# Two-layer decoder trunk on one core: another order inside the three turns between row-wise sums and the next products

## The chip, the core and the metric

The kernel runs on one core of one Trainium2 chip. The metric is the device time of one execution in microseconds (us). The core has five engines that run on their own and meet at semaphores: PE (TensorE: matrix products and transposes), DVE (VectorE: elementwise work and sums), ACT (ScalarE: activations, copies, square sums), POOL (unused here but for constants) and SP (it issues the DMAs). The "granted clock" in the profile is the share of full speed that PE is given.

## The reference

Two layers, 256 tokens, 2048 columns. Cut to what matters here:

```python
for l in range(DEPTH):
    mod = c_act @ w_ada[l] + b_ada[l]
    shift_a, scale_a, gate_a, shift_m, scale_m, gate_m = split(mod, 6)
    h = rms_norm(x, g_pre_mix[l]) * (1 + scale_a) + shift_a
    y = token_mixer(h, ...)                   # one projection h @ W_in, mLSTM and attention, @ W_out
    x = x + gate_a * rms_norm(y, g_post_mix[l])
    h = rms_norm(x, g_pre_mlp[l]) * (1 + scale_m) + shift_m
    y = square(relu(h @ w_up[l])) @ w_down[l]
    x = x + gate_m * rms_norm(y, g_post_mlp[l])
return x
```

## The kernel before

**Products.** Every weight tile is loaded as float32 (`raw`, by SP's queue, six buffers) and split into a high part (`whi`, an ACT copy to the product format) and a low part (`wlo`, DVE: raw minus high). Activations are kept as high and low parts too (`ht...`). A product is a sum of three: high by high, high by low, low by high. A `Unit` is 512 output columns, accumulated in two PSUM banks; a slab is two 128-row weight tiles of it. `split_hi` and `split_lo` issue the two halves of a split (and first the DMA of a later tile), `take` hands the oldest split slab on.

**Turns.** A turn stands wherever a row-wise norm must be finished before the next product can start: after the output projection (to the up products `up`) in both layers, and after layer 0's down products (to layer 1's `vm` and `kva`). There are three in the run. The 256 tokens are two halves of 128 (`tok` 0 and 1), and PE works on the last columns of half 1 while DVE and ACT finish half 0. For each half the order is:

1. `evac`: the last 512 columns leave PSUM: ACT takes their square sum (`jko`, or `jkd` in the second turn), DVE multiplies by the gate (`yg`; in the second turn it first adds into `ys` and the product goes back into the PSUM bank `dn`). `branch` then makes two more sums over these columns: DVE the product sum of branch and residual, whose elementwise output is thrown away into a spare place (`waste`), ACT the square sum of the branch (`jkb...`).
2. `gain`: the reciprocal root of the branch's mean square: DVE reduces four sums (`sst...`), ACT takes the root (`rp..._y`), DVE makes the reciprocal and one step of Newton's method.
3. `root_after`: from the branch's sums (`sum3...`) the mean square of the new residual, and its reciprocal root (`rn..._y`).
4. `step(c, tok)`: x += branch * root, for 512 columns `c`. `scale`: `xn` = x * root. `group(g, tok)`: four PE transposes of `xn` into a PSUM bank (`pst...`), four ACT shifts and scales (`hf...`), an ACT copy to the high part, a DVE subtraction for the low part.

`group_fast`, used once in each turn, for group 0 of half 1, has two PSUM banks; ACT writes the high part straight from PSUM, DVE makes the shifted value again and subtracts.

While half 1 goes through 1 to 4, PE has the first two slabs of the next unit for half 0, and then products whose result nobody reads (`idle`, here called fillers). In a turn (`strict["on"]`) each engine runs in exactly the order in which the code is written; elsewhere a scheduler, which goes by its own cost estimates, sets the order of each engine.

In the rows `up0_0_1` is layer 0, unit 0, half 1; `pstm0_0_1` the transposes of group 0, half 1; `hi0_3h` and `hi0_3l` (and so `hi_5l` in the profile, where digits are cut) are high and low parts of weight slabs that lie in other pools. Pinned instructions carry the line of the wrapper, L63, so names tell them apart.

Of the kernel before, what the change touches and what calls it, by code (L numbers as in the profile page):

```python
# [39 lines left out]
def hymba_kernel(ctx: ExitStack, tc: tile.TileContext, x_d, c_d, cols_d, cons_d, wada_d,  # L40
# [95 lines left out]
        hold["ada"] = last.ins  # L136
        return y

    def rsqrt_one(ssq, n_over, name):

        h, y, t = [smp.tile([P, 1], F32, tag=f"rs_{a}", name=f"{name}_{a}") for a in "vyt"]
        A.activation(y, ssq, AF.Sqrt, bias=eps, scale=1.0 / n_over)
        V.tensor_scalar(h, ssq, -0.5 / n_over, -0.5 * EPS, ALU.mult, ALU.add)
        V.reciprocal(y, y)
        V.tensor_scalar(t, y, y, h, ALU.mult, ALU.mult)
        V.scalar_tensor_tensor(y, t, 1.5, y, ALU.add, ALU.mult)
        return y
# [195 lines left out]
    class Unit:  # L343
# [23 lines left out]
        def slabs_by_token(self):  # L367
# [3 lines left out]
            for tok in range(2):  # L371
                for s in four:
                    if tok == 0:
                        side()
                    self.mm(s, toks=(tok,))

        def run(self, deep=0):

            self.slabs(self.nk // 2 - deep)
            for _ in range(deep):  # L380
                st["ahead"] += 1
                self.slabs(1)
            st["ahead"] = LA + 1
            return self.ps
# [63 lines left out]
    class PreNorm:  # L448
# [3 lines left out]
            self.tag, self.l, self.vsc, self.vsh, self.yg, self.ssy = tag, l, vsc, vsh, yg, ssy  # L452
            self.xn, self.groups, self.r, self.sums = {}, {}, {}, {}

        def gain(self, tok):

            tot = smp.tile([P, 1], F32, tag="ssq1", name=f"sst{self.tag}_{tok}")
            V.tensor_reduce(tot, self.ssy[:, tok, :], AX.X, ALU.add)
            return rsqrt_one(tot, D, f"rp{self.tag}_{tok}")

        def sums_of(self, tok):
            if tok not in self.sums:
# [73 lines left out]
        def group_fast(self, g, tok, between):

            hh, hl, mods, hf = self.begin(g, tok)
            ps = [xalloc(f"pst{self.tag}_{g}_{tok}_{i}") for i in range(2)]
            pk = [ps[k // 2][:, (k % 2) * P:(k % 2 + 1) * P] for k in range(4)]  # L540
            for k in range(4):
                T.transpose(pk[k], self.xn[g, tok][:, k * P:(k + 1) * P], ident)
            for k, (gc, sc) in enumerate(mods):
                A.activation(hh[:, k, :], pk[k], AF.Identity, bias=sc, scale=gc)
            between()
            for i in range(2):
                kk = slice(2 * i, 2 * i + 2)
                for k in range(2 * i, 2 * i + 2):
                    V.tensor_scalar(hf[:, k, :], pk[k], mods[k][0], mods[k][1], ALU.mult, ALU.add)
                V.tensor_tensor(hl[:, kk, :], hf[:, kk, :], hh[:, kk, :].bitcast(F32), ALU.subtract)  # L550
            xdone(2)

        def begin(self, g, tok):
            tag, l = self.tag, self.l
            ada_until(l, self.vsc, self.vsh, n=4 * g + 4)
# [68 lines left out]
            T.matmul(ps, w[:, 0, 0:P], w[:, 1, :], start=True, stop=True)  # L624
        xdone()

    def turn(units, evac, early, nrm, make, staged=None):

        s0 = st["mm"]
        units[0].slabs(1)
        split_to(s0 + 7)
        rest = []
        for i, u in enumerate(units[1:]):
            if early is not None and i == 3:
                early(0)
            side()  # L640
            rest.append((u, take()))
            u.mm(rest[-1][1], toks=(0,))
            split_to(s0 + 8 + (early is not None))
        strict["on"] = True
        for u, slab in rest[:5]:
            u.mm(slab, toks=(1,))
        ahead = st["split"] > s0 + 8

        evac(0)
        r0 = nrm.gain(0)  # L650
        if not ahead:
            split_hi()
        nrm.root_after(0, r0)
        nrm.step(0, 0, r0)
        nrm.scale(0, (0,), ())
        if early is not None:
            early(1, 1)
        nrm.step(1, 0, r0)
        nrm.scale(0, (1,), ())
        if not ahead:  # L660
            split_lo()
        split_hi()
        split_lo()
        steps = nrm.group(0, 0)
        for u, slab in rest[5:]:
            u.mm(slab, toks=(1,))
        for f in steps[:3]:
            f()
        if early is not None:
            early(1, 2)  # L670
        steps[3]()

        evac(1)
        steps = nrm.group(1, 0)
        unit = make[0]()
        four = [take() for _ in range(2)]
        for slab in four:
            unit.mm(slab, toks=(0,))
        idle_products(four[0][2], 12)
        r1 = nrm.gain(1)  # L680
        steps[0]()
        nrm.root_after(1, r1)
        steps[1]()
        steps[2]()
        nrm.step(0, 1, r1)
        nrm.scale(1, (0,), ())
        nrm.step(1, 1, r1)
        nrm.scale(1, (1,), ())
        split_hi()
        steps[3]()  # L690
        nrm.group_fast(0, 1, split_lo)
        four.append(take())
        unit.mm(four[2], toks=(0,))
        steps = nrm.group(1, 1)
        unit.mm(four[0], toks=(1,))
        unit.mm(four[1], toks=(1,))
        split_hi()
        for f in steps:
            f()
        split_lo()  # L700
        for tok, r in ((0, r0), (1, r1)):
            for c in (2, 3):
                nrm.step(c, tok, r)
        four.append(take())
        unit.mm(four[3], toks=(0,))
        for slab in four[2:]:
            unit.mm(slab, toks=(1,))
        units = [unit]
        strict["on"] = False
        hold["hi"], hold["lo"], hold["ada"] = [strict["last"][e] for e in (A, V, V)]  # L710
        for tok in range(2):
            nrm.scale(tok, range(2, 4))
        if staged:
            order, wide, small, done = staged
            xnT = {g: wide.tile([P, 4, S], F32, tag="sl", name=f"xnT{nrm.tag}_{g}") for g in (2, 3)}
            for tok in range(2):
                nrm.turn_in(xnT, tok, 2)
            strict["last"].clear()
            for m in make[1:]:
                units.append(m())  # L720
                units[-1].slabs(4)
            for e in range(4, 8):
                nrm.modulate(e, xnT, small)
                for u in order:
# [30 lines left out]
    for l in range(DEPTH):  # L755
# [454 lines left out]
        def evac_out(ps, c, tok):  # L1210
            yg[c][tok] = ytile(f"yg{L}_{c}_{tok}")
            square_sum(ps[tok], ssy[:, tok, c:c + 1], f"jko{L}_{c}_{tok}")
            V.tensor_tensor(yg[c][tok], ps[tok], gps[l, GTA][:, CH[c]], ALU.mult)
            hT2.branch(tok, c, ps[tok])
            for k in ((0, 1), (2, 3), (), ())[c]:
                hT2.old(tok, k)

# [37 lines left out]

        sT_ = {}
        ysum = [[None, None] for _ in range(4)]
        ssm_ = smp.tile([P, 2, 4], F32, tag="ssy", name=f"ssm_{L}")
        nxt = PreNorm(f"a{l + 1}", l + 1, SCA, SHA, ysum, ssm_) if l + 1 < DEPTH else PreNorm("f", l, 0, 0, ysum, ssm_)

# [54 lines left out]
        def up_done(u, un):  # L1315
            tups[u] = Task((evac_up if u else evac_up_tokens)(un, u))


        tc.keep_in_program_order(A.activation(smp.tile([P, 1], F32, tag="ssq1", name=f"table{L}"), eps, AF.Sqrt))
        ups = turn([un] * 8, lambda tok: evac_out(un.ps, 3, tok), None, hT2,  # L1320
                   [lambda u=u: Unit(f"up{L}_{u}", ("up", l, u), KT, hT2, body_ws if u else body_xs, u > 1)
                    for u in range(NUP[l])], None if l else (LAST, sp, rp, up_done))
        if l:
            for u, un in enumerate(ups):
                un.slabs(4)
# [10 lines left out]
        def evac_down(ps, e, c, tok, part=0):  # L1336
# [7 lines left out]
                if e == 7:  # L1344
                    square_sum(yt, ssm_[:, tok, c:c + 1], f"jkd{L}_{c}_{tok}")
            if e == 7 and part != 1:
                o, waste = yt, ps[tok]
                if c == 3:

                    o, waste = ps[tok], yt  # L1350
                V.tensor_tensor(o, yt, gps[l, GTM][:, CH[c]], ALU.mult)
                ysum[c][tok] = o
                if l + 1 < DEPTH:
                    nxt.branch(tok, c, waste)
                    for k in ((0, 1), (2, 3), (), ())[c]:
                        nxt.old(tok, k)

# [45 lines left out]

        if l + 1 < DEPTH:
            hT = nxt
            starts = turn([previous] * 4 + [un] * 4, evac_last, lambda *a: evac_down(previous.ps, 7, 2, *a), hT,
                          [lambda: Unit(f"vm0{l + 1}", ("in", l + 1, UV0), KT, hT, body_xs),
                           lambda: Unit(f"kva{l + 1}", ("in", l + 1, UKV), KT, hT, body_mix)])
        else:
            un.slabs_by_token()  # L1410
            strict["on"] = True
# [95 lines left out]
```

## Time and profile before

| | |
|---|---|
| Time, 3 runs | 2214.14 us median (2212.89 to 2217.28) |
| The profiled execution: time, span | 2213.18 us, 2211.4 us |
| Busy: PE, DVE, ACT | 97%, 78%, 50% |
| Mean granted clock | 0.992 |
| The turns (from half 1's last products to the transposes of the last groups) | 413.72 to 433.29, 1133.10 to 1156.01, 1485.26 to 1506.64 us |

Rows of a timeline give the start, the duration, the engine, the line, the operation, what it writes and reads, shapes, a count, and in brackets how long the engine had been idle and who released it. In a row of several instructions the duration is that of all; PE's instructions overlap, so a product of 0.39 us is followed by the next much sooner. Rows of windows give the stretch, its length, busy time and number of instructions of PE, its weight loads, DVE, ACT and POOL, then the granted clock, the DMA share and GB/s.

### The profile page before, as it was taken

How to read it: one execution, taken by the hardware profiler on the slowest of the kernel's cores; microseconds unless marked ns; L12 is line 12 of the kernel's file. 1: busy time of each engine (PE TensorE's matmuls, PEld its weight loads, DVE VectorE, ACT ScalarE, POOL GpSimd, SP SyncE). 2: the span in 40 equal slices, each digit the busy share in tenths (PEclk: the TensorE clock that was granted, in tenths of full speed). 3: DMA queues.
4: the chain of work that ended last, by engine and by line, in shares of the span. 5: the costliest groups of instructions: out<-in, count | busy, mean ns of one | idle time of the engine just before them, and what ended most of it. 6: DMA issues, size and time to landing. Idle time of an engine off the chain costs nothing.

```text
span 2211.4 us, 29963 instructions
## 1 busy us (share of the span) xinstructions
PE 2144.2 (97%) x11694; PEld 1834.2 (83%) x11694; DVE 1728.0 (78%) x2393; ACT 1116.0 (50%) x1645; POOL 1.4 (0%) x15
## 2 busy tenths in 40 slices
PE   6889999999999999999999999999999999999998
PEld 5779777798888888888879987788888888888886
DVE  7989999887888888888677898967566767555656
ACT  4256765645444444444565576666443444444434
POOL 0000000000000000000000000000000000000000
PEclk9999999999999999999999999999999999999999
DMA  9998689598889898888638866755666667655552
GB/s 375 388 372 301 232 313 347 209 365 309 309 322 340 305 336 322 318 313 322 207 112 338 315 229 245 257 202 194 236 228 233 231 230 267 210 191 190 191 191 76
DMA packets 82351, 589.88 MB, mean 267 GB/s; under 512 B 9185, under 2 KB 9633, under 8 KB 10785
## 3 DMA queue, kind: packets, MB, share of 16 engines
q1 hardware_dynamic: 82210, 587.98, 72.8%
q8 instruction: 91, 1.49, 0.3%
q14 instruction: 50, 0.41, 0.0%
HBM read 585.81 MB, written 2.13 MB: 266 GB/s over the span
## 4 chain that ended last, share of the span: by engine, by line
PE 85%; DVE 10%; ACT 3%; issue 1%; DMA 1%; SPq 0%; DVEq 0%; ACTq 0%
PE dn L389 31%; PE up L414 17%; PE up L416 9%; PE up L389 5%; PE op L389 5%; DVE raw L244 4%; PE om L389 3%; PE qa L389 2%; DVE wlo L285 2%; PE qm L389 2%; PE vm L389 2%; PE km L389 1%; PE kva L389 1%; PE op L63 1%; PE up L63 1%
## 5 line engine op out<-in xcount | busy, mean ns | idle before, releaser
L285 DVE TENSOR_TENSOR wlo<-raw,whi 128x1024 fp32r<-128x1024 f32 x699 | 849.4, 1222 | 389.3 <-ACT whi L275 388.0
L275 ACT ACTIVATE whi<-raw 128x1024 fp32r<-128x1024 f32 x699 | 737.2, 1059 | 813.5 <-PE dn L389 333.2
L414 PE MATMUL up<-htm,whi 128*128 128x512 f32 x1664 | 571.9, 394 | 0.0
L244 DVE SCALAR_TENSOR_TENSOR raw<-raw,cact 128x2048 f32<-128x2048 f32 x192 | 437.5, 2284 | 9.6 <-DMA raw<-in_wada_dram 9.3
L416 PE MATMUL up<-htm,wlo 128*128 128x256 f32 x1664 | 444.8, 277 | 0.0
L389 PE MATMUL dn<-whi,sh 128*128 128x512 f32 x1004 | 391.1, 390 | 1.1 <-DVE r L1288 1.1
L389 PE MATMUL dn<-whi,sl 128*128 128x512 f32 x1004 | 390.7, 389 | 0.0
L389 PE MATMUL dn<-wlo,sh 128*128 128x512 f32 x1004 | 390.7, 389 | 0.0
L414 PEld LDWEIGHTS up<-htm,whi 128*128 128x128 f32 x1664 | 305.8, 188 | 64.3
L416 PEld LDWEIGHTS up<-htm,wlo 128*128 128x128 f32 x1664 | 312.6, 188 | 9.0
L389 PEld LDWEIGHTS dn<-whi,sh 128*128 128x128 f32 x1004 | 188.4, 188 | 41.1 <-DVE r L1288 1.6
L389 PEld LDWEIGHTS dn<-wlo,sh 128*128 128x128 f32 x1004 | 188.5, 188 | 39.2
L389 PEld LDWEIGHTS dn<-whi,sl 128*128 128x128 f32 x1004 | 188.5, 188 | 38.8 <-DVE sl L1310 0.2
L389 PE MATMUL op<-whi,ct 128*128 128x512 f32 x432 | 137.1, 396 | 0.7 <-DVE ct L1162 0.7
L389 PE MATMUL vm<-whi,hta 128*128 128x512 f32 x224 | 78.0, 431 | 21.4 <-ACT whi L275 18.7
L389 PEld LDWEIGHTS op<-whi,ct 128*128 128x128 f32 x432 | 80.7, 188 | 19.1 <-DVE ct L1162 1.4
L389 PE MATMUL qa<-hta,whi 128*128 128x256 f32 x512 | 93.6, 284 | 0.0
L389 PE MATMUL up<-htm,whi 128*128 128x256 f32 x512 | 92.8, 284 | 0.2 <-ACT whi L275 0.2
L389 PE MATMUL op<-wlo,ct 128*128 128x512 f32 x216 | 84.2, 394 | 5.4 <-DVE wlo L285 5.4
L389 PE MATMUL om<-whi,hta 128*128 128x512 f32 x256 | 82.0, 401 | 0.0
L389 PEld LDWEIGHTS up<-htm,whi 128*128 128x128 f32 x512 | 80.0, 192 | 1.1 <-ACT whi L275 0.7
L389 PEld LDWEIGHTS qa<-hta,whi 128*128 128x128 f32 x512 | 79.8, 192 | 0.9 <-issue 0.7
(412 smaller groups left out, 2485.3 us busy)
## 6 DMA issues: line engine op xcount, KB each, us to landing
raw<-in_wada_dram SPq DMA_DIRECT2D x192, 1024.0 KB, 7.0
raw<-in_wdn_dram SPq DMA_DIRECT2D x128, 1024.0 KB, 4.9
raw<-in_wup_dram SPq DMA_DIRECT2D x120, 1024.0 KB, 5.2
raw<-in_win_dram SPq DMA_DIRECT2D x56, 1024.0 KB, 5.4
raw<-in_wout_dram SPq DMA_DIRECT2D x32, 1024.0 KB, 5.5
raw<-in_wst_dram SPq DMA_DIRECT2D x16, 1024.0 KB, 7.4
raw<-in_wsu_dram SPq DMA_DIRECT2D x8, 1024.0 KB, 5.4
gp<-gdr SPq DMA_DIRECT2D x4, 1024.0 KB, 5.0
```

What stands on the lines that cost most here:

```text
L63: made = tc.keep_in_program_order(make(*args, **kw))
L244: V.scalar_tensor_tensor(w, w, 1.0, cact, ALU.mult, ALU.mult, accum_out=modc[l][:, v, j:j + 1])
L275: A.activation(hi, raw, AF.Copy)
L285: V.tensor_tensor(lo, raw, hi.bitcast(F32), ALU.subtract)
L389: T.matmul(o, a, w, start=not self.started[b], stop=last and i == 2, skip_group_check=True)
L414: T.matmul(u.ps[j], wh[:, cs], u.act.both(kt), start=kt == 0, stop=False, skip_group_check=True)
L416: T.matmul(u.ps[j][:, 0:S], wl[:, cs], xh, start=False, stop=kt == u.nk - 1, skip_group_check=True)
```

## The change

Five things change, all in the turns.

The product sum and the square sum of the last 512 columns (`branch(tok, 3, ...)`) leave `evac` and are issued inside `gain`, between what the root needs and the reciprocal that waits for it. On DVE, first turn, half 1, before and after (`op0_3_1` is the bank thrown into, `sstm` the reduced sum, `rpm` the root):

```order
L63 TENSOR_TENSOR yg0_3_1_3807<-op0_3_1_3619,gp0_2_2584 128x512
L63 SCALAR_TENSOR_TENSOR op0_3_1_3619,sumsm0_1_3257<-yg0_3_1_3807,x_96 128x512
L63 TENSOR_REDUCE sstm0_1_3848<-ssy0_2844 128x1
L63 TENSOR_SCALAR rpm0_1_v_3850<-sstm0_1_3848 128x1
L63 RECIPROCAL rpm0_1_y_3851<-rpm0_1_y_3851 128x1
```

```order
L63 TENSOR_TENSOR yg0_3_1_3807<-op0_3_1_3619,gp0_2_2584 128x512
L63 TENSOR_REDUCE sstm0_1_3843<-ssy0_2844 128x1
L63 TENSOR_SCALAR rpm0_1_v_3845<-sstm0_1_3843 128x1
L63 SCALAR_TENSOR_TENSOR op0_3_1_3619,sumsm0_1_3257<-yg0_3_1_3807,x_96 128x512
L63 RECIPROCAL rpm0_1_y_3846<-rpm0_1_y_3846 128x1
```

The product sum moved from ahead of the reduce to just ahead of the reciprocal; on ACT the root moved ahead of the square sum `jkb` in the same way.

`group_fast` is gone; group 0 of half 1 is an ordinary `group`, so ACT alone shifts. The second `step` and `scale` of half 1 move behind two low parts, and the low part of the following weight slab moves ahead of the last group's. DVE, first turn, from half 1's first `xnm` on, before and then after:

```order
L63 TENSOR_SCALAR xnm0_0_1_3878<-x_96,rnm0_1_y_3867 128x512
L63 SCALAR_TENSOR_TENSOR x_96<-yg0_1_1_3452,rpm0_1_y_3851,x_96 128x512
L63 TENSOR_SCALAR xnm0_1_1_3881<-x_96,rnm0_1_y_3867 128x512
L63 TENSOR_TENSOR htm0_1_3814<-hfm0_1_0_3815,htm0_1_3814 128x4x128
L63 TENSOR_TENSOR hi0_5l_3886<-raw121_3559,hi0_5h_3885 128x1024
L63 TENSOR_SCALAR hfm0_0_1_3889<-pstm0_0_1_0_3890,modc0_106 128x128 x2
L63 TENSOR_TENSOR htm0_0_3782<-hfm0_0_1_3889,htm0_0_3782 128x2x128
L63 TENSOR_SCALAR hfm0_0_1_3889<-pstm0_0_1_1_3891,modc0_106 128x128 x2
L63 TENSOR_TENSOR htm0_0_3782<-hfm0_0_1_3889,htm0_0_3782 128x2x128
L63 TENSOR_TENSOR htm0_1_3814<-hfm0_1_1_3913,htm0_1_3814 128x4x128
L63 TENSOR_TENSOR wlo107_3932<-raw121_3559,whi107_3931 128x1024
```

```order
L63 TENSOR_SCALAR xnm0_0_1_3881<-x_96,rnm0_1_y_3865 128x512
L63 TENSOR_TENSOR htm0_1_3811<-hfm0_1_0_3812,htm0_1_3811 128x4x128
L63 TENSOR_TENSOR hi0_5l_3878<-raw121_3559,hi0_5h_3877 128x1024
L63 SCALAR_TENSOR_TENSOR x_96<-yg0_1_1_3452,rpm0_1_y_3846,x_96 128x512
L63 TENSOR_SCALAR xnm0_1_1_3903<-x_96,rnm0_1_y_3865 128x512
L63 TENSOR_TENSOR htm0_0_3782<-hfm0_0_1_3885,htm0_0_3782 128x4x128
L63 TENSOR_TENSOR wlo107_3931<-raw121_3559,whi107_3930 128x1024
L63 TENSOR_TENSOR htm0_1_3811<-hfm0_1_1_3912,htm0_1_3811 128x4x128
```

Four shifts (two rows of two) are gone, `hi0_5l` stands two places and `wlo107` one place nearer to the first `xnm`.

The first two slabs of the next unit are multiplied with all high activations first and the low ones last (`two_slabs`), and the fillers stand in two runs, 10 and 5 in the first and third turn and 14 and 5 in the second, where there was one run of 12. PE, first turn, before and then after:

```order
L63 MATMUL up0_0_0_3821<-hi0_4h_3778,htm0_0_3782 128x512 x2
L63 MATMUL up0_0_0_3821<-hi0_4l_3779,htm0_0_3782 128x512
L63 MATMUL up0_0_0_3821<-hi0_4h_3778,htm0_0_3782 128x512
L63 MATMUL idle106_3835<-hi0_3h_3754 128x512 x12
L63 MATMUL pstm0_0_1_0_3890<-cons_98,xnm0_0_1_3878 128x128 x2
L63 MATMUL pstm0_0_1_1_3891<-cons_98,xnm0_0_1_3878 128x128 x2
L63 MATMUL up0_0_0_3821<-hi0_5h_3885,htm0_1_3814 128x512
L63 MATMUL up0_0_0_3821<-hi0_5l_3886,htm0_1_3814 128x512
```

```order
L63 MATMUL up0_0_0_3818<-hi0_3h_3754,htm0_0_3782 128x512 x2
L63 MATMUL up0_0_0_3818<-hi0_4h_3778,htm0_0_3782 128x512 x2
L63 MATMUL idle106_3832<-hi0_3h_3754 128x512 x10
L63 MATMUL pstm0_0_1_3886<-cons_98,xnm0_0_1_3881 128x128 x4
L63 MATMUL idle106_3891<-hi0_3h_3754 128x512 x5
L63 MATMUL up0_0_0_3818<-hi0_5h_3877,htm0_1_3811 128x512
L63 MATMUL up0_0_0_3818<-hi0_5l_3878,htm0_1_3811 128x512
```

The second run of fillers stands between the transposes and the third slab's products. Behind the turns the scheduler sets some instructions in another order too: four early products of the next up unit go behind the last transposes, and in layer 1's mixing stage many DVE and ACT instructions change places by a few. The order of the DMAs stays, but for one small load of layer 1 and one of its gate rows.

```diff
-    def rsqrt_one(ssq, n_over, name):
+    def rsqrt_one(ssq, n_over, name, between=None):
         A.activation(y, ssq, AF.Sqrt, bias=eps, scale=1.0 / n_over)
         V.tensor_scalar(h, ssq, -0.5 / n_over, -0.5 * EPS, ALU.mult, ALU.add)
+        if between is not None:
+            between()
         V.reciprocal(y, y)
...
+        def two_slabs(self, slabs, tok):
+            for late in range(2):
+                for unit, kt0, hi, lo in slabs:
+                    assert unit == self.unit
+                    for k in range(2):
+                        h, l_ = [a[:, TK[tok]] for a in self.act(kt0 + k)]
+                        wh, wl = hi[:, k, :], lo[:, k, :]
+                        self.products(self.ps[tok], tok, ((l_, wh),) if late else ((h, wh), (h, wl)), kt0 + k)
...
-        r0 = nrm.gain(0)
+        r0 = nrm.gain(0, lambda: nrm.branch(0, 3, waste(0)))
...
-        for slab in four:
-            unit.mm(slab, toks=(0,))
-        idle_products(four[0][2], 12)
-        r1 = nrm.gain(1)
+        unit.two_slabs(four, 0)
+        idle_products(four[0][2], pauses[0])
+        r1 = nrm.gain(1, lambda: nrm.branch(1, 3, waste(1)))
         steps[0]()
         nrm.root_after(1, r1)
         steps[1]()
         steps[2]()
+        split_hi()
         nrm.step(0, 1, r1)
         nrm.scale(1, (0,), ())
+        steps[3]()
+        split_lo()
+        steps = nrm.group(0, 1)
+        idle_products(four[0][2], pauses[1])
+        for f in steps[:3]:
+            f()
         nrm.step(1, 1, r1)
         nrm.scale(1, (1,), ())
-        split_hi()
         steps[3]()
-        nrm.group_fast(0, 1, split_lo)
         four.append(take())
         unit.mm(four[2], toks=(0,))
         steps = nrm.group(1, 1)
-        unit.mm(four[0], toks=(1,))
-        unit.mm(four[1], toks=(1,))
+        unit.two_slabs(four[:2], 1)
         split_hi()
+        split_lo()
         for f in steps:
             f()
-        split_lo()
```

The rest of the diff passes `waste` and `pauses` through, and skips `branch` for column block 3 in the two `evac` functions.

More of the change, by code (lines that the diff above doesn't have):

```diff
@@ L453, in __init__, with gain @@
             self.xn, self.groups, self.r, self.sums = {}, {}, {}, {}
-        def gain(self, tok):
+        def gain(self, tok, between=None):
             tot = smp.tile([P, 1], F32, tag="ssq1", name=f"sst{self.tag}_{tok}")
             V.tensor_reduce(tot, self.ssy[:, tok, :], AX.X, ALU.add)
-            return rsqrt_one(tot, D, f"rp{self.tag}_{tok}")
+            return rsqrt_one(tot, D, f"rp{self.tag}_{tok}", between)
         def sums_of(self, tok):
@@ L534, in whole_group @@
                 f()
[L536 to L551, printed above, removed]
         def begin(self, g, tok):
@@ L625, in idle_products, with turn @@
         xdone()
-    def turn(units, evac, early, nrm, make, staged=None):
+    def turn(units, evac, early, waste, nrm, make, pauses, staged=None):
         s0 = st["mm"]
@@ L1213, in evac_out @@
             V.tensor_tensor(yg[c][tok], ps[tok], gps[l, GTA][:, CH[c]], ALU.mult)
-            hT2.branch(tok, c, ps[tok])
+            if c < 3:
+                hT2.branch(tok, c, ps[tok])
             for k in ((0, 1), (2, 3), (), ())[c]:
@@ L1257, in hymba_kernel @@
         ysum = [[None, None] for _ in range(4)]
+        spoil = {}
         ssm_ = smp.tile([P, 2, 4], F32, tag="ssy", name=f"ssm_{L}")
@@ L1319, in hymba_kernel @@
         tc.keep_in_program_order(A.activation(smp.tile([P, 1], F32, tag="ssq1", name=f"table{L}"), eps, AF.Sqrt))
-        ups = turn([un] * 8, lambda tok: evac_out(un.ps, 3, tok), None, hT2,
+        ups = turn([un] * 8, lambda tok: evac_out(un.ps, 3, tok), None, lambda tok: un.ps[tok], hT2,
                    [lambda u=u: Unit(f"up{L}_{u}", ("up", l, u), KT, hT2, body_ws if u else body_xs, u > 1)
-                    for u in range(NUP[l])], None if l else (LAST, sp, rp, up_done))
+                    for u in range(NUP[l])], (10, 5), None if l else (LAST, sp, rp, up_done))
         if l:
@@ L1346, in evac_down @@
             if e == 7 and part != 1:
-                o, waste = yt, ps[tok]
+                o = yt
                 if c == 3:
-                    o, waste = ps[tok], yt
+                    o, spoil[tok] = ps[tok], yt
                 V.tensor_tensor(o, yt, gps[l, GTM][:, CH[c]], ALU.mult)
@@ L1353, in evac_down @@
                 if l + 1 < DEPTH:
-                    nxt.branch(tok, c, waste)
+                    if c < 3:
+                        nxt.branch(tok, c, ps[tok])
                     for k in ((0, 1), (2, 3), (), ())[c]:
@@ L1405, in hymba_kernel @@
             hT = nxt
-            starts = turn([previous] * 4 + [un] * 4, evac_last, lambda *a: evac_down(previous.ps, 7, 2, *a), hT,
+            starts = turn([previous] * 4 + [un] * 4, evac_last, lambda *a: evac_down(previous.ps, 7, 2, *a), spoil.get, hT,
                           [lambda: Unit(f"vm0{l + 1}", ("in", l + 1, UV0), KT, hT, body_xs),
-                           lambda: Unit(f"kva{l + 1}", ("in", l + 1, UKV), KT, hT, body_mix)])
+                           lambda: Unit(f"kva{l + 1}", ("in", l + 1, UKV), KT, hT, body_mix)], (14, 5))
         else:
```

## The prediction

> **What bounds the kernel now.** I read the page first, then who waited for whom on PE, then busy time by stretch, then the three turns engine by engine.
>
> ```profile
> PE 2144.2 (97%) x11694; PEld 1834.2 (83%) x11694; DVE 1728.0 (78%) x2393; ACT 1116.0 (50%) x1645; POOL 1.4 (0%) x15
> ```
>
> PE is busy for 97% of the span, so only PE's gaps, and products that are no work, can be won. The longest of PE's waits that lie in the turns:
>
> ```profile
> PE up L63 <- DVE hi_5l L63: 4.2, 2, 2.1
> ...
> PE vm L63 <- DVE wlo L63: 2.4, 2, 2.0
> ```
>
> Columns: total, times, longest; up and vm are the products of the next unit, and hi_5l and wlo are low parts of its weights, made by DVE. The stretches by windows (length, PE busy, PEld, DVE, ACT, POOL, granted clock, DMA) are the three turns, from the second token half's last product to the transposes of the last two column groups, and two stages behind them:
>
> ```profile
> 413.72:433.29 19.57, 16.50 (x78) 12.74 (x77) 16.45 (x39) 13.85 (x27) 0.00 (x0) 1.00 0.32 105
> 1133.10:1156.01 22.91, 17.99 (x74) 13.46 (x72) 18.54 (x42) 14.50 (x32) 0.20 (x2) 0.93 0.28 92
> 1485.26:1506.64 21.38, 18.77 (x78) 14.86 (x76) 16.78 (x39) 13.86 (x27) 0.00 (x0) 0.84 0.28 98
> 433.30:700.00 266.70, 266.70 (x1547) 235.56 (x1546) 225.34 (x244) 125.97 (x148) 0.00 (x0) 1.00 0.87 324
> 1180.00:1470.00 290.00, 289.43 (x1818) 252.72 (x1817) 244.83 (x444) 179.28 (x325) 0.00 (x0) 1.00 0.76 276
> ```
>
> Behind the turns PE has no gap (266.70 of 266.70), so what a turn gains should stay gained. The first and the third turn do the same work, yet the third takes 1.81 us more: its mean clock is 0.84. The reason shows in windows of 3.41 us:
>
> ```profile
> 418.86:422.27 3.41, 1.81 (x10) 1.00 (x8) 3.20 (x7) 3.20 (x8) 0.00 (x0) 1.00 0.00 0
> 1139.01:1142.42 3.41, 1.90 (x10) 1.29 (x9) 2.99 (x12) 2.52 (x6) 0.00 (x0) 1.00 0.00 0
> 1142.42:1145.83 3.41, 1.41 (x8) 1.00 (x7) 3.34 (x7) 2.58 (x6) 0.10 (x1) 1.00 0.00 0
> 1145.83:1149.24 3.41, 3.41 (x12) 2.71 (x11) 1.39 (x4) 1.31 (x4) 0.10 (x1) 0.50 0.02 5
> 1490.57:1493.98 3.41, 1.67 (x9) 0.90 (x7) 3.20 (x6) 3.21 (x7) 0.00 (x0) 1.00 0.00 0
> ```
>
> After the window in which PE was busy 1.41 us, the next is granted 0.50, and after the one with 1.67 the third turn is slow: its mean of 0.84 over 21.38 us makes (1-0.84) x 21.38 / 0.5 = 6.8 us at 0.50, two windows. After 1.81 and 1.90 the clock stays at 1.00. The two slow spells begin at 1145.83 and 1493.98, 348.15 us or 102 times 3.413 apart, so the edges are fixed in time and it is luck where a gap falls. A slow window holds 12 products where a full one of the same length has 15 (3.41/0.227, below), transposes and the window's start aside; at half clock 3.41 us cost at most 1.7.
>
> **The change, step by step.** PE in the first turn:
>
> ```profile
> 416.90 2.88 PE L63 MATMUL idle<-hi_3h 128*128 128x512 f32 x12
> 420.33 0.66 PE L63 MATMUL pstm<-cons,xnm 128*128 128x128 f32 x4 [0.55 <-DVE xnm L63]
> ...
> 423.32 0.50 PE L63 MATMUL up<-hi_5l,htm 128*128 128x512 f32 x1 [2.10 <-DVE hi_5l L63]
> ...
> 424.59 0.60 PE L63 MATMUL pstm<-cons,xnm 128*128 128x128 f32 x4
> ...
> 428.40 0.74 PE L389 MATMUL up<-htm,whi 128*128 128x256 f32 x4 [0.24 <-ACT whi L275]
> 429.31 0.50 PE L63 MATMUL up<-wlo,htm 128*128 128x512 f32 x1 [0.18 <-DVE wlo L63]
> ...
> 433.29 1.91 PE L62 MATMUL pstm<-cons,xnm 128*128 128x128 f32 x16
> ```
>
> Twelve fillers span 2.88, with 0.39 for the last, so products follow each other every (2.88-0.39)/11 = 0.227 us; four transposes take about 0.36. DVE there, second token half:
>
> ```profile
> 414.64 0.69 DVE L63 TENSOR_TENSOR yg<-op,gp 128x512 f32<-128x512 f32 x1 [0.18 <-ACT jko L63]
> 415.36 0.70 DVE L63 SCALAR_TENSOR_TENSOR op<-yg,x 128x512 f32<-128x512 f32 x1
> 415.98 0.15 DVE L63 TENSOR_REDUCE sstm<-ssy 128x1 f32<-128x4 f32 x1
> ...
> 416.49 0.17 DVE L63 RECIPROCAL rpm_y<-rpm_y 128x1 f32<-128x1 f32 x1 [0.17 <-ACT rpm_y L63]
> ...
> 419.79 0.49 DVE L63 TENSOR_SCALAR xnm<-x,rnm_y 128x512 f32<-128x512 f32 x1
> 420.19 0.74 DVE L63 SCALAR_TENSOR_TENSOR x<-yg,rpm_y,x 128x512 f32<-128x512 f32 x1
> ...
> 421.44 0.69 DVE L63 TENSOR_TENSOR htm<-hfm,htm 128x512 fp32r<-128x512 f32 x1
> 422.05 1.22 DVE L63 TENSOR_TENSOR hi_5l<-raw,hi_5h 128x1024 fp32r<-128x1024 f32 x1
> ...
> 428.04 1.22 DVE L63 TENSOR_TENSOR wlo<-raw,whi 128x1024 fp32r<-128x1024 f32 x1
> ```
>
> The sum moved into the root's wait: the product sum holds DVE for a slot of 0.62 (415.36 to 415.98). Without it ahead, the reduce starts one such slot after yg, at 415.26. From reduce to reciprocal before were 0.51, of which 0.17 was waiting for ScalarE's root; so the two small instructions take 0.34, the root is there at 415.77, and the product sum fills the wait from 415.60. The reciprocal follows at 415.60 + 0.62 = 416.22 instead of 416.49. The chain to xnm gains 0.27: 420.28 becomes 420.01, and the transposes start at 420.06. In the first half the same gain is hidden in this turn and the third: PE still has the last unit's products to do there.
>
> The order behind xnm: before, the second x update and its xnm came ahead of the low parts (1.25 us, 420.19 to 421.44). Now htm's low part runs at 419.92, hi_5l from 420.52 to 421.74, then the x update and xnm, done at 422.99. Between them PE has transposes until 420.47 and five fillers until 421.60. Its first hi_5 product starts there and the second needs hi_5l just as it lands. So the 2.10 wait and the 0.55 before it become a gap of 0.9 (ten fillers end near 419.2) plus 1.14 of fillers: the second transposes come at 423.04, not 424.59, which is 1.55 earlier.
>
> Shifting by ScalarE alone takes four 0.36 us shifts and a half-split low part off DVE and costs ScalarE a copy:
>
> ```profile
> 420.81 1.50 ACT L63 ACTIVATE htm<-pstm,modc 128x128 fp32r<-128x128 f32 x4 [0.18 <-PE pstm L63]
> 422.19 1.07 ACT L63 ACTIVATE whi<-raw 128x1024 fp32r<-128x1024 f32 x1
> 426.77 0.63 ACT L63 ACTIVATE htm<-hfm 128x512 fp32r<-128x512 f32 x1
> ```
>
> Four shifts end at 422.04, the copy at 422.70, whi at 423.65: ahead of PE's need at 423.40. The low part is on DVE until 423.58, and low-part products come last, at 425.2, so they wait for nothing. Then wlo runs at 423.72 instead of 428.04, where it was queued behind a low part that waited for ScalarE. PE's halt there (428.0 to 429.31, of which four products moved in from the next unit filled 0.47) goes. From 423.40 there are 12+6+12 = 30 products: 423.40 + 30 x 0.227 = 430.2. With the four products done later, 430.7 against 433.29: **2.6 us**. The last x updates then run from 426.4 to 429.1, so xnm of the last groups is there at 430.0; that is what is late next, by a margin of 0.2.
>
> Third turn: the same schedule takes 430.7 - 413.72 = 17.0 in place of 21.38, **4.4 us**, 1.8 of it clock.
>
> Second turn. It has a longer chain, bound by DVE from the first half on:
>
> ```profile
> 1134.25 0.50 PE L63 MATMUL vm<-hi_h,hta 128*128 128x512 f32 x1 [0.55 <-ACT hta L63]
> ...
> 1142.19 0.66 PE L63 MATMUL psta<-cons,xna 128*128 128x128 f32 x4 [1.51 <-DVE xna L63]
> ...
> 1137.52 0.60 ACT L63 ACTIVATE jkba<-dn 128x512 bf16<-128x512 f32 x1 [0.77 <-DVE ys L63]
> 1138.02 0.20 ACT L63 ACTIVATION_READ_ACCUMULATOR jkba<-dn 128x1 f32 x1
> ...
> 1138.43 0.16 DVE L63 RECIPROCAL rpa_y<-rpa_y 128x1 f32<-128x1 f32 x1 [0.68 <-ACT rpa_y L63]
> ...
> 1139.01 0.16 DVE L63 TENSOR_REDUCE sum3a<-sumsa 128x3 f32<-128x12 f32 x1
> ```
>
> ScalarE's square sum jkba waits for DVE's product sum, and the root stood behind it, hence DVE's 0.68. Now the root goes first, and the product sum starts 0.36 later than it did (reduce and the small instruction ahead of it). jkba, still behind it, starts at 1137.88 and its sum is read by 1138.58. The step that needs it, the reduce of the three sums, stood at 1139.01. It can now start at 1138.63: 0.38 earlier, and not 0.6, since jkba bounds it. The first half's 0.38 passes on to the second, so xna comes 0.76 earlier: transposes at 1141.43. The first products start at 1133.87, and with the low parts last they no longer stop for hta's low part (an estimate: 12 products in 2.9). Fourteen fillers end near 1139.9: a gap of 1.5. After that, transposes to 1141.85, five fillers to 1142.99, hi products as wlo lands (1143.11), 6 products, transposes to 1144.75, 30 products: 1151.6 against 1156.01, the end of its row among the stretches: **4.4 us**, some 1.6 of it clock.
>
> The moved DMAs: each load is issued when a raw tile is free; wlo frees one 4.3 us earlier in the first turn (428.04 to 423.72) and PE needs it 2.6 us earlier, so the load queue gains. In layer 1's mixing stage the scheduler set another order for DVE, ScalarE and a few products; PE lacks only 0.57 us there in all, so I take 0. The ends are -0.6 and the longest wait of ScalarE for a softmax maximum there, 3.1:
>
> ```profile
> ACT s L840 <- DVE nm L837: 5.0, 4, 3.1
> ```
>
> Sum: 2.6 + 4.4 + 4.4 = 11.4. The profiled execution took 2213.18 for a span of 2211.4, 0.96 under the median of 2214.14. 2213.18 - 11.4 = 2201.8.
>
> **Rivals.** First: the clock still falls. PE's gap of 1.5 in the second turn leaves about 1.9 busy in a window, as in the row at 1139.01, which was let pass; 0.2 us more would not be. Price: 1.7 for one spell (half of 3.41), to 3.4 with a second, so 2203.5 to 2205.2. [...]
>
> Second: the turn's end is set by the x updates of the last columns, not by PE's waits; then only clock is won, 1.8 + 1.6 = 3.4, and the time is 2209.8, near no change. Against it: these updates are pure DVE work queued behind low parts that come earlier too.
>
> Third, on the other side: layer 1's new order makes PE wait for splits. Where a unit of values waits for them now, PE has this row:
>
> ```profile
> PE vm L389 <- ACT whi L275: 18.7, 7, 3.9
> ```
>
> At that price the time is 2201.8 + 18.7 = 2220.5. It decides from 16 us on (11.4 and the 4.4 that a measurement tells apart). Against it: ScalarE is busy 179 of 290 us there.
>
> **How the numbers follow.** Forecast 0.68, clock 0.16, last columns 0.08, layer 1's order 0.08 (half of it under the full price). About 0.2%, 4.4 us, can be told from no change: faster 0.88, same 0.07, slower 0.05. The range begins at 2198, where the gaps left (0.9 + 1.5 + 0.9) vanish as well, and ends at 2208, with the clock rival and a 3.1 wait in layer 1 both (2205.2 + 3.1); the last-columns case and the full price lie outside.
>
> **What would show it.** Right: turns of about 17, 18.5 and 17 us; no 2 us wait for hi_5l or wlo, a gap near 1.5 ahead of the second turn's transposes, clock 1.00 throughout all three. Wrong: 0.50 in a turn, PE waiting for xnm ahead of the sixteen transposes, or waits on whi or wlo between 1170 and 1460.

## The result, and the profile after

Four executions of the changed kernel took 2203.15 us in the median (2201.68 to 2205.25), four of the kernel before beside them 2214.28 (2212.89 to 2217.28). The ratio is 0.9944, with a 95% interval from 0.9932 to 0.9956. The forecast was 2201.8 with a range of 2198 to 2208. The profiled execution took 2203.41 us for a span of 2201.6, 9.8 us less than the span before. The medians are 11.1 apart; the rows below account for the 9.8 between the two profiled executions.

The page's first part, then PE's waits in the turns:

```profile
PE 2142.8 (97%) x11707; PEld 1835.8 (83%) x11707; DVE 1723.0 (78%) x2378; ACT 1114.4 (51%) x1646; POOL 1.4 (0%) x15
```

```profile
PE psta L63 <- DVE xna L63: 1.3, 1, 1.3
...
PE pstm L63 <- DVE xnm L63: 1.2, 2, 0.6
...
PE vm L63 <- ACT hta L63: 0.5, 1, 0.5
```

The waits for `hi_5l` (4.2) and `wlo` (2.4) are gone from the list. What is left in the turns is 1.3, twice 0.6, and 0.5. The three turns by windows, from the same second transposes to the same last ones:

```profile
416.04:432.60 16.56, 15.97 (x76) 12.81 (x75) 14.21 (x33) 14.11 (x28) 0.00 (x0) 1.00 0.36 128
1132.59:1151.52 18.93, 17.11 (x80) 13.60 (x79) 16.83 (x37) 14.79 (x32) 0.20 (x2) 1.00 0.33 115
1479.83:1496.36 16.53, 15.95 (x77) 12.81 (x76) 14.17 (x33) 14.11 (x28) 0.00 (x0) 1.00 0.37 127
```

The granted clock is 1.00 in all three (0.93 and 0.84 before in the second and third), and the first and third turn now take the same time. PE in the first turn:

```profile
419.25 2.43 PE L63 MATMUL idle<-hi_3h 128*128 128x512 f32 x10
422.27 0.66 PE L63 MATMUL pstm<-cons,xnm 128*128 128x128 f32 x4 [0.59 <-DVE xnm L63]
422.68 1.41 PE L63 MATMUL idle<-hi_3h 128*128 128x512 f32 x5
423.92 0.39 PE L63 MATMUL up<-hi_5h,htm 128*128 128x512 f32 x1
424.15 0.40 PE L63 MATMUL up<-hi_5l,htm 128*128 128x512 f32 x1
...
425.32 0.60 PE L63 MATMUL pstm<-cons,xnm 128*128 128x128 f32 x4
```

The product with `hi_5l` follows 0.23 behind its neighbour, where PE had stood for 2.10. DVE in the same stretch:

```profile
417.57 0.15 DVE L63 TENSOR_REDUCE sstm<-ssy 128x1 f32<-128x4 f32 x1
417.75 0.15 DVE L63 TENSOR_SCALAR rpm_v<-sstm 128x1 f32<-128x1 f32 x1
417.82 0.69 DVE L63 SCALAR_TENSOR_TENSOR op<-yg,x 128x512 f32<-128x512 f32 x1
...
418.43 0.16 DVE L63 RECIPROCAL rpm_y<-rpm_y 128x1 f32<-128x1 f32 x1
...
422.73 1.22 DVE L63 TENSOR_TENSOR hi_5l<-raw,hi_5h 128x1024 fp32r<-128x1024 f32 x1
...
426.12 1.23 DVE L63 TENSOR_TENSOR wlo<-raw,whi 128x1024 fp32r<-128x1024 f32 x1 [0.26 <-ACT whi L63]
```

The product sum now fills the wait for the root: the reciprocal shows no idle time ahead of it (0.17 before).

Where the 9.8 us are, by how far the changed kernel is ahead. The stretches run from one turn's last transposes to the next turn's second ones.

| stretch | before | after | gain |
|---|---|---|---|
| start to first turn | 413.72 | 416.04 | -2.32 |
| first turn | 19.57 | 16.56 | 3.01 |
| to second turn | 699.81 | 699.99 | -0.18 |
| second turn | 22.91 | 18.93 | 3.98 |
| to third turn (layer 1's mixing) | 329.25 | 328.31 | 0.94 |
| third turn | 21.38 | 16.53 | 4.85 |
| to the end of the span | 704.8 | 705.2 | -0.48 |

The turns give 11.84. Four up products that stood inside the first and the third turn now stand behind them, and take 0.49 and 0.48 back there. In the -0.18 these 0.49 are nearly made up by 0.40 that belong to the second turn, whose start has moved (see below, on the chain through the root); 0.09 stays open. The two entries that the change did not aim at, -2.32 and 0.94, are followed up below.

### The profile page after: what moved, and what is told of

Read it like the earlier page. It is cut to its first block, busy times and chain, and to the rows that moved or that the text cites. A ratio compares the mean times of both kernels' runs of the same rounds, so it can differ in the third digit from the quotient of the medians.

```text
span 2201.6 us, 29985 instructions
## 1 busy us (share of the span) xinstructions
PE 2142.8 (97%) x11707; PEld 1835.8 (83%) x11707; DVE 1723.0 (78%) x2378; ACT 1114.4 (51%) x1646; POOL 1.4 (0%) x15
## 4 chain that ended last, share of the span: by engine, by line
PE 87%; DVE 9%; ACT 2%; issue 1%; DMA 1%; SPq 0%; DVEq 0%; ACTq 0%
PE dn L402 31%; PE up L427 17%; PE up L429 9%; PE up L402 5%; PE op L402 5%; DVE raw L247 4%; PE om L402 3%; PE qa L402 2%; PE vm L402 2%; PE qm L402 2%; PE km L402 2%; DVE wlo L288 2%; PE kva L402 1%; PE up L63 1%; PE op L63 1%
## 5 line engine op out<-in xcount | busy, mean ns | idle before, releaser
L402 PE MATMUL vm<-whi,hta 128*128 128x512 f32 x224 | 79.3, 437 | 21.1 <-ACT whi L278 18.5
```

The lines of the kernel that those rows point to most:

```text
L402: T.matmul(o, a, w, start=not self.started[b], stop=last and i == 2, skip_group_check=True)
```

## The experiments

Ten kernels ran, in three groups, each timed in five rounds beside the kernel before on the same chip. The turns are from one profile each, in us; they repeat well (the changed kernel, run again in the last group, has 16.56, 18.91 and 16.54), so differences of 0.1 can be read from them, while the intervals of the ratios are some 5 us wide (0.0024 of 2214). The kernel before had medians of 2216.40, 2215.91 and 2215.99 in the three groups (e1 to e4, e5 to e8, e9 and e10), so a median of the table is to be read with its ratio, not against 2214.28.

| kernel | turns | their sum | median | ratio, 95% |
|---|---|---|---|---|
| before | 19.57, 22.91, 21.38 | 63.86 | 2214.28 | 1 |
| changed | 16.56, 18.93, 16.53 | 52.02 | 2203.15 | 0.9944 (0.9932 to 0.9956) |
| e1 before + fillers | 19.57, 22.01, 19.63 | 61.21 | 2212.68 | 0.9982 (0.9973 to 0.9991) |
| e2 no second run of fillers | 16.56, 18.85, 16.58 | 51.99 | 2203.96 | 0.9946 (0.9934 to 0.9959) |
| e3 no fillers | 18.09, 20.63, 18.57 | 57.29 | 2209.08 | 0.9968 (0.9956 to 0.9981) |
| e4 x update first | 17.74, 20.06, 17.75 | 55.55 | 2207.61 | 0.9960 (0.9948 to 0.9973) |
| e5 sums back in `evac` | 16.92, 19.44, 16.92 | 53.28 | 2205.98 | 0.9952 (0.9940 to 0.9965) |
| e6 DVE shifts too | 16.66, 18.93, 16.66 | 52.25 | 2204.81 | 0.9946 (0.9932 to 0.9959) |
| e7 slab by slab | 16.56, 18.95, 16.54 | 52.05 | 2204.43 | 0.9944 (0.9932 to 0.9957) |
| e8 low part late | 17.97, 20.41, 17.98 | 56.36 | 2207.66 | 0.9960 (0.9948 to 0.9973) |
| e9 zeros at the start | 16.57, 18.91, 16.55 | 52.03 | 2202.39 | 0.9944 (0.9931 to 0.9958) |
| e10 changed, again | 16.56, 18.91, 16.54 | 52.01 | 2202.79 | 0.9942 (0.9929 to 0.9954) |

### e1: the clock alone

The kernel before, with nine fillers behind its `group_fast`:

```diff
         nrm.group_fast(0, 1, split_lo)
+        idle_products(four[0][2], 9)
```

> The kernel before, with nine more fillers between group_fast's transposes and the third slab's first product, in the wait of 2.1 us for its low part; nothing else. Theory A (the clock is a term of its own, set by how busy PE is in a fixed window of 3.41 us): the three turns run at a clock of 1.00 and take about 19.6, 21.3 and 19.6 us; the time is 2 to 4 us under the kernel before, near 2210. Theory B (only the new order of DVE and ScalarE counts, and slow spells do not hang on fillers): spells at 0.50 appear in a turn as before and the time is that of before, 2214.

The second turn and the wait that grew in it:

```profile
1133.97:1155.98 22.01, 18.38 (x82) 13.83 (x81) 18.55 (x42) 14.39 (x32) 0.21 (x2) 1.00 0.29 95
```

```profile
1151.97 0.50 PE L63 MATMUL vm<-wlo,hta 128*128 128x512 f32 x1 [1.15 <-DVE wlo L63]
```

The clock stays at 1.00 and the third turn wins 1.75, as booked (1.8). The second wins 0.90 and not 1.6: at full clock PE comes earlier to `wlo`, which is no earlier, and waits 1.15 for it (0.4 before). So the clock alone is worth 2.65 us in this profile, and 0.18% in the times; the rest of the gain, some 9 us in the turns, needs the other parts.

### e2 and e3: the fillers

```diff
-        idle_products(four[0][2], pauses[1])
```

> The changed kernel without the second run of fillers (5 in each turn); the first runs of 10, 14 and 10 stay. The five fillers (1.1 us) become a wait. Theory A: in the first and third turn PE is then quiet for 0.6 + 1.2 us, about 1.6 busy in the worst window, at the edge between 1.67 (fell) and 1.81 (let pass), so the clock falls or not by luck; in the second turn 1.3 + 1.2 us are quiet and it falls in most executions, 1.7 us each time: 2203 to 2208, the turns 16.6, 18.9 and 16.5 where the clock stays. Theory B: 2203 and no spell.

e3 takes out this line and the one with `pauses[0]`.

> The changed kernel without any filler. PE waits about 3.0 (second turn 4.6) us for xnm and 1.2 for the third slab's low part. Theory A: the clock falls in all three turns, one or two windows each, 1.7 to 3.4 us a turn: 2208 to 2213, most of the gain gone. Theory B: 2203, since no filler is work and DVE's chain sets the turn.

Without the second run the turns are as long as with it and the clock stays at 1.00: PE then waits for `hi_5l` and `wlo` (0.84 and 0.81), in place of fillers that covered nothing else. That it holds the clock was not seen in the profiled execution; the fall that was expected for most executions of e2's second turn did not come in it. Without any, the clock falls in all three turns. Windows of e3 in the first and the second turn, each row 3.41 us, the length of the slow stretch from 1145.83 to 1149.24 in the kernel before:

```profile
419.46:422.87 3.41, 1.70 (x8) 1.06 (x6) 2.92 (x16) 2.73 (x9) 0.00 (x0) 1.00 0.63 264
422.87:426.29 3.42, 1.43 (x7) 1.06 (x8) 3.31 (x5) 2.99 (x7) 0.00 (x0) 1.00 0.00 0
426.29:429.70 3.41, 3.41 (x11) 2.75 (x10) 2.44 (x4) 2.54 (x5) 0.00 (x0) 0.50 0.00 0
...
1139.68:1143.09 3.41, 0.25 (x2) 0.00 (x0) 2.72 (x15) 2.56 (x8) 0.00 (x0) 1.00 0.15 62
1143.09:1146.50 3.41, 1.90 (x6) 1.39 (x7) 3.38 (x6) 2.60 (x6) 0.00 (x0) 0.50 0.00 0
1146.50:1149.92 3.42, 3.42 (x11) 2.74 (x11) 2.64 (x4) 2.53 (x6) 0.20 (x2) 0.50 0.00 0
```

The column before the last two is the granted clock. Behind the window with PE busy for 1.70 us the next is at 1.00, behind those with 1.43 and 0.25 it is at 0.50, and behind the slow window with 1.90 a second slow one follows. With the first run of fillers alone the clock stayed at 1.00 in e2's profile, and without both runs the turns cost 5.27 more in sum (57.29 against 52.02). The fillers delay nothing: the first turn's transposes come 6.23 behind its start with them and without (422.27 - 416.04, and 424.02 - 417.79 in e3). The second run alone was not tried.

### e4: the second x update ahead of the low parts, as it was

```diff
         steps[1]()
         steps[2]()
+        nrm.step(1, 1, r1)
+        nrm.scale(1, (1,), ())
...
-        nrm.step(1, 1, r1)
-        nrm.scale(1, (1,), ())
```

> The changed kernel with the second x update and its xnm back ahead of the two low parts on DVE, as before; all else as changed. Theory A (PE waits for DVE's low part of the third slab): that low part comes 1.25 us later and PE waits for it again, turns of about 17.8, 20.2 and 17.8, 2207, more if the longer gap lets the clock fall. Theory B (the x updates of the last columns set the turn's end): turns as they are now, 16.6, 18.9 and 16.5, 2203.

```profile
423.10 0.66 PE L63 MATMUL pstm<-cons,xnm 128*128 128x128 f32 x4 [0.59 <-DVE xnm L63]
426.09 0.50 PE L63 MATMUL up<-hi_5l,htm 128*128 128x512 f32 x1 [0.94 <-DVE hi_5l L63]
```

PE's wait for `hi_5l` is back, 0.94 behind five fillers, and the turns are 1.18, 1.13 and 1.22 longer: DVE's update and scale of 1.25 us go straight onto PE's path. This order is worth 3.5 us.

### e5: the sums back in evac

```diff
-        r1 = nrm.gain(1, lambda: nrm.branch(1, 3, waste(1)))
+        nrm.branch(1, 3, waste(1))
+        r1 = nrm.gain(1)
```

and the same for half 0.

> The changed kernel with the product sum and the square sum of the last columns back ahead of the root, as before; all else as changed. Theory A (the sum is on the chain to xnm): xnm comes 0.27 us later in the first and third turn and 0.76 in the second, and PE's gap ahead of the transposes grows by as much: turns of about 16.8, 19.3 (and its start 0.2 to 0.4 later) and 16.8, in all 1.3 us, 2204.5. Theory B (the gain comes from the order behind xnm and the clock alone): no change, 2203.

The first and the second turn's transposes in e5:

```profile
423.78 0.66 PE L63 MATMUL pstm<-cons,xnm 128*128 128x128 f32 x4 [1.00 <-DVE xnm L63]
```

```profile
1143.54 0.66 PE L63 MATMUL psta<-cons,xna 128*128 128x128 f32 x4 [1.73 <-DVE xna L63]
```

The gaps go from 0.59 to 1.00 and from 1.31 to 1.73, the turns get 0.36, 0.51 and 0.39 longer: 1.3 in sum. The second turn's start also comes 0.39 later behind the first product of layer 0's last columns (`dn<-hi`; 10.39 against 10.00), so the order is worth some 1.65, more than the 1.3 expected.

### e6 and e7: two parts that were worth next to nothing

e6 gives group 0 back its two PSUM banks, ACT's high part straight from PSUM and DVE's four shifts (in the places that the changed kernel has for them). e7 multiplies the first slabs in the old order:

```diff
-        unit.two_slabs(four, 0)
+        for slab in four:
+            unit.mm(slab, toks=(0,))
...
-        unit.two_slabs(four[:2], 1)
+        for slab in four[:2]:
+            unit.mm(slab, toks=(1,))
```

> The changed kernel with half 1's first group shifted by both engines again (ScalarE straight to the high part, DVE four shifts and two subtractions at the place of the one low part). Theory A (ScalarE alone is what lets wlo and the low part come in time): DVE has 1.6 us more ahead of wlo; wlo then ends just when PE needs it, so a turn loses 0 to 0.4: 2203 to 2204.5. Theory B (it is the bulk of the gain behind xnm): 1.6 a turn, 2208.

> The changed kernel without the low-part products last: the first two slabs are multiplied slab by slab. Theory A: in the second turn PE stops 0.5 us for hta's low part ahead of the fillers, and the gap behind the fillers shrinks by the same; in half 1 the low part is there in time; so nothing changes, 16.6, 18.9 and 16.5, 2203. Theory B (as the prediction's sum had it, PE's stop for that low part is won): the second turn takes 19.3 to 19.4.

With DVE shifting again the turns cost 0.10, 0 and 0.13 more. With the old product order PE stops in the second turn for `hta`'s low part, but then it comes later to the transposes, which it had to wait for anyway:

```profile
1136.03 0.74 PE L63 MATMUL vm<-hi_h,hta 128*128 128x512 f32 x2 [0.42 <-DVE hta L63]
...
1142.37 0.66 PE L63 MATMUL psta<-cons,xna 128*128 128x128 f32 x4 [0.60 <-DVE xna L63]
```

The gap of 1.31 became 0.42 + 0.60 and a few tenths of later products: this stop ahead of a wait that DVE's chain sets cost nothing (18.95 against 18.93 for the turn).

### e8: the next low part behind the last group's again

```diff
         split_hi()
-        split_lo()
         for f in steps:
             f()
+        split_lo()
```

> The changed kernel with the low part of the fourth slab's weights (wlo) behind the last group's steps again. Theory A: wlo waits on DVE for a low part that waits for ScalarE and starts 2.6 us later; PE's product needs it at once and waits about 1.3 us: turns of 17.9, 20.2 and 17.9, 2207. Theory B (the x updates of the last columns end the turn): the updates come no later than now, so 2203.

The first and the second turn:

```profile
430.42 0.50 PE L63 MATMUL up<-wlo,htm 128*128 128x512 f32 x1 [0.17 <-DVE wlo L63]
```

```profile
1150.11 0.50 PE L63 MATMUL vm<-wlo,hta 128*128 128x512 f32 x1 [1.16 <-DVE wlo L63]
```

The wait for `wlo` is back. The turns are 1.41, 1.48 and 1.45 longer; in the first and the third the scheduler again fills 0.47 with four early up products, which leaves some 0.94, 1.48 and 0.98, 3.4 us in all.

### e9 and e10: the 2.3 us at the start

The code ahead of the first turn is the same in both kernels, yet the changed one came there 2.32 us later. e9 adds, in the changed kernel, eight products with a tile of zeros ahead of the start stage's last iteration; e10 is the changed kernel again.

```diff
+                    if e == 7:
+                        for _ in range(8):
+                            T.matmul(first[0].ps[0], zero, seen[0][:, 1, :], start=False, stop=False, ...)
```

> The changed kernel plus eight products with a tile of zeros, added into the vm bank ahead of the last iteration of the start stage, in PE's wait for the first high part there (1.50 us before, 3.87 in the changed kernel). All else is in the same order. In the changed kernel's profile the clock fell at 144.95, behind that wait, and the first turn began 2.32 us later than in the kernel before (416.04 against 413.72), though the code up to there is the same. Theory A (this fall is why): no 0.50 between 144 and 149 us, the first turn's second transposes start at 413.7 to 414.7, the three turns stay at 16.6, 18.9 and 16.5, and the median is 0 to 2.4 us under the changed kernel's, 2201 to 2203. Rival (the stage is bound by the loads and the splits, and PE's clock only shows it): the turn begins at 416 to 418 as before, time 2203 to 2205; if the zeros themselves delay the stage by 8 x 0.227, up to 2205.

> The changed kernel once more, unaltered, beside the run with the zeros. Theory A: whether the clock falls near 145 us is set by where the window edges lie in that execution; if it falls, the first turn begins near 416, if not, near 413.7. Turns 16.6, 18.9 and 16.5, time 2202 to 2205. Rival (the 2.3 us belong to the changed kernel whatever the clock does there): the first turn begins near 416 in this execution even if no window between 140 and 150 us is at 0.50.

PE's first products of that iteration, in the kernel before, the changed one, e10 and e9 (there with the zeros):

```profile
145.33 0.73 PE L389 MATMUL vm<-whi,hta 128*128 128x512 f32 x2 [1.50 <-ACT whi L275]
```

```profile
145.22 1.22 PE L402 MATMUL vm<-whi,hta 128*128 128x512 f32 x2 [3.87 <-ACT whi L278]
```

```profile
146.63 0.73 PE L402 MATMUL vm<-whi,hta 128*128 128x512 f32 x2 [2.32 <-ACT whi L278]
```

```profile
143.57 2.00 PE L777 MATMUL vm<-whi,zero 128*128 128x512 f32 x8
146.63 0.73 PE L404 MATMUL vm<-whi,hta 128*128 128x512 f32 x2 [1.06 <-ACT whi L279]
```

The two products take 1.22 instead of 0.73 where the clock has just fallen. From the start of this row to the first turn's second transposes it is 268.39 in the kernel before, in e1 and in e9 (413.72 - 145.33, 414.56 - 146.17, 415.02 - 146.63), the three without a fall there; in the other nine profiles the clock falls between 144.9 and 148.8 and it is 269.97 to 272.21. So the fall costs 1.6 to 3.8 us, 2.43 of it in the changed kernel's profile. Theory A holds for this, and e9 speaks against the rival (late whatever the clock does). e10 does not test it, since the clock fell there too.

But the turn begins at 415.02 in e9, not at 413.7 to 414.7 as expected: the row's own start lies between 145.01 and 146.78 in the twelve profiles. It comes 16.34 or 16.35 after the same row of the iteration before (128.99 in the kernel before, 128.67 in e8, 130.28 in e9), whatever PE's clock did in between. That fits loads and splits that set the pace here, but no run changed them. Both effects are smaller than the spread of the times: e9's 2202.39 and e10's 2202.79 can't be told apart, though e9 has the shortest span of all profiles (2200.3).

That the fall came in every profile of a changed kernel without zeros and in neither of the two others may still be chance. PE's wait is 1.50 in those two and 2.31 or more in the nine. In the two, PE had spent two slow windows in the iteration ahead (128.66 to 135.48 in the kernel before) and so came later; nothing in the code there differs.

## Why the prediction came out

**The turns.** The first was put at 2.6, the second at 4.4, the third at 4.4; measured are 2.52, 4.38 and 4.37. The first is 3.01 less the 0.49 of the four products that now stand behind it: from its last transposes to the first down product it is 82.12 before, 82.61 after, and 82.13 in e8, where the four still stand in the turn. The third is 4.85 less the 0.48 behind it. The second is the 3.98 of the table and the 0.40 by which its start moved. The schedule that was laid out row by row held: the first turn's second transposes were to come 9.32 behind the turn's start (423.04 - 413.72), and came at 9.28 (425.32 - 416.04); the gap ahead of the first ones was put at 0.9 and was 0.59, that of the second turn at 1.5 and was 1.31. Undone alone, the x update behind the low parts is worth 3.5 (e4), the early low part 3.4 (e8), the sum in the root's wait 1.65 (e5).

**The chain through the root.** In the first turn it was to gain 0.27; transposes came 6.61 behind the turn's start and come now 6.23 behind it, 0.38. In the second it was to gain 0.38 in each half and 0.76 in all. From the first product of layer 0's last columns (`dn<-hi`, at 1122.70 before and 1122.59 after) to half 1's transposes it takes 19.49 before and 18.61 after: 0.88, some 0.44 in each half. DVE no longer waits for the root (0.68 before), and both halves wait for `jkba`, the bound that the prediction named:

```profile
1125.20 0.16 DVE L63 RECIPROCAL rpa_y<-rpa_y 128x1 f32<-128x1 f32 x1
...
1126.10 0.17 DVE L63 TENSOR_REDUCE sum3a<-sumsa 128x3 f32<-128x12 f32 x1 [0.24 <-ACT jkba L63]
...
1138.01 0.17 DVE L63 TENSOR_REDUCE sum3a<-sumsa 128x3 f32<-128x12 f32 x1 [0.23 <-ACT jkba L63]
```

Inside the turn only 0.48 of it shows (9.09 to 8.61), because the turn's own start has moved. The first half's gain reaches PE ahead of that start, where PE's wait for the first half's `xna` is gone, in the kernel before and then in the changed one:

```profile
1129.84 0.66 PE L63 MATMUL psta<-cons,xna 128*128 128x128 f32 x4 [0.18 <-DVE xna L63]
```

```profile
1129.39 0.60 PE L63 MATMUL psta<-cons,xna 128*128 128x128 f32 x4
```

The turn's start lay 10.40 behind the same `dn<-hi` product and lies 10.00 behind it now; in e5, with the sums back, it is 10.39 again. The prediction left the start where it was and booked both halves inside the turn. Counted so, the 18.93 are 18.53, where 18.5 had been laid out.

**The parts priced inside those sums.** The clock was put at 1.8 + 1.6; alone it is worth 1.75 + 0.90 (e1), since the wait for `wlo` takes the place of slow products. Low-part products last were to spare a stop in the second turn: they do, and it is worth nothing (e7). Shifts by ACT alone are worth 0 to 0.13 per turn (e6). The second run of fillers is not what kept the clock in e2's profile. None of these four wrong prices changes the total, because each turn was costed as a whole schedule.

**The clock rival** did not come true: in the lowest window of the changed kernel's turns PE is busy for 2.11 of 3.41. The rival took 0.2 less than the 1.9 of the row at 1139.01 as enough for a fall. No run shows such an edge. Behind e3's window of 1.70 the clock is at 1.00 and behind the one of 1.67 in the kernel before at 0.50, but in the start stage of the changed kernel's own profile it is at 1.00 behind a window of 1.75 (76.68 to 80.09) and at 0.50 behind one of 1.81 (45.97 to 49.38). Without the transposes the windows do not sort either: the 1.81 of e2's second turn (1141.23 to 1144.64), less the transposes' whole row of 0.66, leaves 1.15, and the next is at 1.00, while the 1.81 just named has no transpose in it, nor has a window of 1.18 in e3's third turn, and behind both the next is at 0.50. The rows of e3:

```profile
1487.84:1491.25 3.41, 1.18 (x6) 0.62 (x4) 2.92 (x14) 2.77 (x9) 0.00 (x0) 1.00 0.48 204
1491.25:1494.66 3.41, 2.60 (x8) 1.90 (x9) 3.22 (x5) 2.52 (x6) 0.00 (x0) 0.50 0.00 0
```

So neither way of counting PE's busy time sorts the windows, and what does is not shown by these runs.

**The last columns** did not bind: no wait for `xnm` stands at the sixteen transposes, whose row begins right behind the last product. It was close: DVE's last `xnm` ends at 432.30, 0.30 ahead of that row, where 0.2 had been put.

**Layer 1's new order** was put at 0, with a price of up to 18.7 as a rival. It gained 0.94. PE is busy nearly throughout in both kernels; its idle time went from 0.63 to 0.44, since a wait of 0.2 for ACT's `sT` is gone. The largest piece is in these rows, of the kernel before and then of the changed one:

```profile
1342.18 0.34 PE L1030 MATMUL pscol<-cons,rows 4*128 4x4 f32 x3
1342.45 0.73 PE L389 MATMUL om<-whi,hta 128*128 128x512 f32 x2
1343.12 0.69 PE L1054 MATMUL pg<-rows,cons 4*128 4x256 f32 x2
...
1344.87 0.28 PE L1030 MATMUL pscol<-cons,rows 4*128 4x4 f32 x2
...
1346.34 0.40 PE L389 MATMUL om<-wlo,hta 128*128 128x512 f32 x1
```

```profile
1337.38 0.47 PE L1030 MATMUL pscol<-cons,rows 4*128 4x4 f32 x5
1337.71 0.67 PE L1054 MATMUL pg<-rows,cons 4*128 4x256 f32 x2
...
1340.94 0.39 PE L402 MATMUL om<-wlo,hta 128*128 128x512 f32 x1
```

The same work, five small products, two of `pg` and eleven of `om` up to the last row, takes 4.16 before and 3.56 after, and PE goes once to the small products and back, not three times. The scheduler put them so, and nobody meant it. All twelve profiles agree: where the five stand in one row (changed, e4, e5, e7, e9, e10) the way from the second turn to the third takes 328.09 to 328.31, where they stand three and two (before, e1, e2, e3, e6, e8) 328.96 to 329.26. The last 0.15 were not followed up, and the order itself was not tried alone, so that it is the cause is argued from the rows and not shown.

**The sum.** 2.52 + 4.38 + 4.37 is 11.27, where 11.4 was forecast, so the turns came out by the schedule that was laid out. Layer 1's 0.94, put at 0, comes on top; the start, which the prediction did not look at, takes 2.32 back in this profile (2.43 for the fall of the clock, less a start of the row that is 0.11 earlier), and 0.09 is open: 9.8. That the median (2203.15) lies only 1.35 from the forecast is in part luck: two things outside the turns, one for and one against, were not seen, and the start differs from one execution to the next.

## What to carry to other kernels

In a stretch where two engines take turns in feeding a third, lay the schedule out row by row to the end of the stretch, and ask of each part what waits behind it: what is won ahead of a wait that another engine's chain sets was worth nothing here (e7, 18.95 against 18.93), while the order of two pieces of work on the engine that is late went straight through (1.13 to 1.22 a turn in e4, 0.94 to 1.48 in e8). A change of order is also to be costed in places where no engine waits: in layer 1's mixing stage the rows with two more visits of PE to small products took 0.60 longer, all of it booked as busy (above; the order was not tried alone). Put the edges of a stretch where the change can't move them, or look at what happened to the edge: a gain that comes ahead of it is booked to the neighbour. And where the profile grants 0.50 anywhere, look at it in several executions before a difference of 2 us is put down to the code: the falls between 144.9 and 148.8 us went with 1.6 to 3.8 here.

## What was not expected of the hardware

The falls of the clock lie on a grid that is fixed in time within an execution: in e3 those at 64.47, 81.53, 98.60, 129.32 and 146.39 us lie 5, 10, 19 and 24 steps of 3.413 us behind the first ((146.39 - 64.47) / 24), and in the kernel before the slow stretches in the turns are one and two steps long (1145.83 to 1149.24, 1493.98 to 1500.80). Short stops of PE stood at the two falls in the turns, in the second and the third turn of the kernel before:

```profile
1145.11 0.51 PE L63 MATMUL vm<-wlo,hta 128*128 128x512 f32 x1 [2.00 <-DVE wlo L63]
```

```profile
1494.86 0.80 PE L63 MATMUL up<-hi_5l,htm 128*128 128x512 f32 x1 [2.09 <-DVE hi_5l L63]
```

Behind the first turn's stop of 2.10 the clock stayed at 1.00. The length of the stop does not tell the three apart. PE's busy time in a window does: 1.41 and 1.67 in the windows ahead of the falls, 1.81 in the first turn's (418.86 to 422.27; 1.88 from 418.79, where steps of 3.4133 us back from 1145.83 put its edge). It holds for these three alone, since 1.81 stands ahead of a fall in the changed kernel's start stage.

In layer 1's mixing stage a visit of PE to small products and back took some 0.3 us with no idle time shown, by an estimate from one place (4.16 less 3.56, for two more visits, above).
